# An encoder trunk on one core: wide products with channels on the output partitions, and the residual kept transposed

## The chip, the cores and the metric

The kernel runs on one core of a Trainium2 chip. The metric is the device time of one execution in microseconds; the reference is computed in float32.

## The reference, cut to what matters

The model has two layers (DEPTH 2), 256 tokens, 1024 channels, 2816 hidden channels. In each layer the same residual `x` passes through three parts:

```
h = rms_norm(x, ffn1_norm);  x = x + 0.5 * (silu(h @ w_gate) * (h @ w_up)) @ w_down
h = rms_norm(x, mix_norm)
s5_u, gla_q, gla_k, gla_v, ..., at_q, at_k, at_v = split(h @ w_in)       # three branches
branches = s5(...), gla(...), attn(...)                                   # 512 columns each
merged = sum over b of sigmoid(h @ w_merge_gate[b] + b_merge_gate[b]) * (branch_b @ w_branch_b)
x = x + merged @ w_out
h = rms_norm(x, ffn2_norm);  x = x + 0.5 * (silu(h @ w_gate) * (h @ w_up)) @ w_down
```

After both layers comes a last `rms_norm`. Over 200 MB of weights are read once.

## The kernel before, in words

Every large product goes through `stream`. It walks over blocks of 512 output columns and chunks of four 128-row tiles of the weights. `load` (lines 193 to 214) brings two such row tiles at a time by DMA, and splits each weight into a high part rounded to float32r (ScalarE, line 209) and a low remainder (VectorE, line 210). Activations are split the same way. `mm3` (lines 216 to 221) then makes one product from three matmuls: high by high, high by low, low by high. The activations of 128 tokens are the stationary operand and 512 columns of weights move, so the result has **tokens on the partitions**: two PSUM tiles of 128 tokens x 512 channels per block, and 6 matmuls per row tile of weights and block.

A product that feeds another product must have its channels on the partitions. With tokens on the partitions this takes TensorE transposes (a matmul with the identity), at four places:

- `norm` (lines 251 to 279) transposes the residual `x` (16 transposes of 128x128, line 263), multiplies by the gain (VectorE, line 265), rounds (ScalarE, line 267) and subtracts (VectorE, line 268). The root of the mean square, `rstd`, is one number per token, thus per partition; it is applied when a product leaves PSUM. There are six such norms, and a last one in `final` that needs no transpose.
- `ffn`'s gate/up product: after each block of 256 hidden channels, each of the two token tiles is transposed by itself (line 298), rounded and subtracted (lines 300, 301).
- q and k of the gated linear attention (`ev_tr`, line 714).
- `merge` (line 1127), ahead of the output projection.

The merge gates (lines 748 to 764) add a bias which varies along the free axis, so it is broadcast to all partitions by a DMA (`bm`, line 757). `s5_glu` (lines 876 to 899) is the one product that has channels on the output partitions already: a 128x128 piece of the weights is stationary and 256 tokens move.

The order on each engine is set by a planner of the framework, from its own estimates of durations and the order in which the program is written. Each engine takes its instructions strictly in that order. `weave` mixes the main product stream with side parts (tables of the S5 recurrence, and the three branches).

Of the kernel before, what the change touches and what calls it, by code (L numbers as in the profile page):

```python
# [38 lines left out]
# main steps before a side part begins, and its steps per main step  # L39
# [12 lines left out]
# columns of the constants: those for the mixer, then those for the tables  # L52
# [4 lines left out]
def constants():  # L57
    """Arrays that depend on shapes alone, one row per partition."""
# [24 lines left out]
def cols(*parts):  # L83
    """Columns of weights [K, N] side by side: for the k tiles [a, z)."""
    def f(a, z):
        res, o = [], 0
        for w, cs in parts:
            res.append((w[a * P:z * P, cs].rearrange("(k p) n -> p k n", p=P), 0, o))
            o += cs.stop - cs.start
        return res  # L90
    return f


def weave(main, sides, up=nullcontext):
    """Emit main; from its step `start` on, `per` steps of a side part after each step of main.
    sides: list of [start, per, generator]. Whatever is left of them comes in the end."""
# [29 lines left out]
class Enc:  # L126
    def __init__(self, tc, ctx, ins, out):
# [15 lines left out]
        self.x = c.tile([P, NT, D], F32, name="x")  # L143
        self.cst = c.tile([P, C_MIX], F32, name="cst")
        self.row = {}
        with tc.high_priority():
            self.vectors("ffn1_norm", eng=nc.scalar)
            for h in range(2):
                for t in range(NT):
                    hs = slice(h * 512, (h + 1) * 512)  # L150
                    nc.scalar.dma_start(self.x[:, t, hs], ins["x"][0, t * P:(t + 1) * P, hs])
# [13 lines left out]
    def vectors(self, *names, eng=None):  # L165
        """Parameters of channels, to partitions: [128 channels, (layer, tile)]"""
        nc = self.nc
        eng = eng or nc.sync
        n = 48 if len(names) > 1 else 16
# [3 lines left out]
        for name in names:  # L173
# [6 lines left out]
            else:  # L180
                eng.dma_start(vec[r:r + DEPTH * KD], self.ins[name].rearrange("l (k p) -> (l k) p", p=P))
                self.row[name] = (vt, r, KD)
# [10 lines left out]
    def load(self, pieces):  # L193
        """pieces: list of (dram AP [partitions, k tiles, columns], first partition, first column)"""
# [21 lines left out]
    def mm3(self, ps, act, w, first, last):  # L216
        """act: (hi, lo) [128 k, 128 tok]; w: (hi, lo) [128 k, n]"""
# [4 lines left out]

    def stream(self, act, nk, blocks, lead=1):
        """act(k, t) -> (hi, lo). blocks: list of (pieces(k0, k1) in k tiles, width, evac(t, ps)).
        The first `lead` blocks take their first chunks together."""
# [3 lines left out]
        ps = {}  # L229
        for b, c in order:  # L230
            pieces, width, evac = blocks[b]
            k0, k1 = chunks[c]
            w = self.load(pieces(k0, k1))
            for t in range(NT):
# [6 lines left out]
            for s in range(0, k1 - k0, SUB):  # L241
                for t in range(NT):
                    for k in range(k0 + s, min(k1, k0 + s + SUB)):
                        self.mm3(ps[b, t][:, :width], act(k, t), w[k - k0], k == 0, k == nk - 1)
            if c == len(chunks) - 1:
                for t in range(NT):
                    evac(t, ps[b, t][:, :width])
            yield

# [1 line left out]
    def norm(self, name, l):  # L251
# [3 lines left out]
        sq = self.st.tile([P, 2, NT], F32, name=f"sq{self.n}", tag="sq")  # L255
# [3 lines left out]
        for c in range(2):  # L259
            for t in range(NT):  # L260
# [4 lines left out]
                nc.vector.tensor_tensor(f, pt, g[:, 4 * c:4 * c + 4].unsqueeze(2).to_broadcast((P, 4, P)), op=ALU.mult)  # L265
                h = hi[:, 4 * c:4 * c + 4, t * P:(t + 1) * P]
                nc.scalar.copy(h, f)  # L267
                nc.vector.tensor_tensor(lo[:, 4 * c:4 * c + 4, t * P:(t + 1) * P], f, h.bitcast(F32), op=ALU.subtract)  # L268
        for c in range(2):
            for t in range(NT):  # L270
                junk = self.t2([P, 512])
                nc.scalar.activation(junk, self.x[:, t, c * 512:(c + 1) * 512], AF.Square,
                                     accum_out=sq[:, c, t:t + 1])
        ms = self.st.tile([P, NT], F32, name=f"ms{self.n}", tag="ms")
        nc.vector.tensor_tensor(ms, sq[:, 0], sq[:, 1], op=ALU.add)
        nc.vector.tensor_scalar(ms, ms, 1.0 / D, EPS, op0=ALU.mult, op1=ALU.add)
        nc.gpsimd.tensor_tensor(rstd, ms, self.mhalf[:, :NT], op=ALU.pow)
        act = lambda k, t: (hi[:, k, t * P:(t + 1) * P], lo[:, k, t * P:(t + 1) * P])
        return act, rstd

    def ffn(self, l, which):
        nc, ins = self.nc, self.ins
        wg, wu, wd = (ins[f"{which}_w_{s}"][l] for s in ("gate", "up", "down"))
        with self.tc.tile_pool(name=f"ffn{which}{l}", bufs=1) as fp:
            self.phase, self.rings = fp, {"ra": 4}
            act, rstd = self.norm(f"{which}_norm", l)
            sh = fp.tile([P, KF, SEQ], F32R, name=f"sTh{which}{l}")
            sl = fp.tile([P, KF, SEQ], F32R, name=f"sTl{which}{l}")

            def evac(b):  # L290
                def f(t, ps):
                    self.n += 1
# [884 lines left out]
```

## Time and profile before

| | |
|---|---|
| time, median of 3 runs | 1378.12 us (1378.01 to 1379.51) |
| span of the profiled execution | 1376.2 us |
| the profiled execution's own time beside its span | not listed; the median of the runs is 1.9 us above the span |
| PE / DVE / ACT busy | 97% / 74% / 51% |
| matmuls, and as many weight loads | 6920 |
| DMA, mean share of 16 engines | 57.5% in the main queue |

PE is TensorE, PEld its weight loads, DVE is VectorE, ACT is ScalarE, POOL is GpSimd. A matmul's duration in the trace includes its way through the array, which overlaps the next one, so the distance from start to start says what a matmul costs in a sequence.

### The profile page before, as it was taken

How to read it: one execution, taken by the hardware profiler on the slowest of the kernel's cores; microseconds unless marked ns; L12 is line 12 of the kernel's file. 1: busy time of each engine (PE TensorE's matmuls, PEld its weight loads, DVE VectorE, ACT ScalarE, POOL GpSimd, SP SyncE). 2: the span in 40 equal slices, each digit the busy share in tenths (PEclk: the TensorE clock that was granted, in tenths of full speed). 3: DMA queues.
4: the chain of work that ended last, by engine and by line, in shares of the span. 5: the costliest groups of instructions: out<-in, count | busy, mean ns of one | idle time of the engine just before them, and what ended most of it. 6: DMA issues, size and time to landing. Idle time of an engine off the chain costs nothing.

```text
span 1376.2 us, 19506 instructions
## 1 busy us (share of the span) xinstructions
PE 1336.0 (97%) x6920; PEld 1061.6 (77%) x6920; DVE 1018.4 (74%) x1826; ACT 698.6 (51%) x1102; POOL 73.5 (5%) x104
## 2 busy tenths in 40 slices
PE   7999999999999999999999999999999999999997
PEld 5878788778787678768877777887787877888886
DVE  5899975779986789996465775457799767655553
ACT  5545345447585355445355454354475754555542
POOL 1020210000100000110000000000001000000000
PEclk9999999999999999999999999999999999999999
DMA  7766666565453366666665646566654533655662
GB/s 227 195 211 224 234 222 179 189 205 198 140 183 122 107 161 206 200 202 221 198 195 173 204 149 204 180 178 202 196 200 134 168 107 122 191 178 186 182 213 76
DMA packets 201201, 249.88 MB, mean 182 GB/s; under 512 B 40856, under 2 KB 134600, under 8 KB 201104
## 3 DMA queue, kind: packets, MB, share of 16 engines
q1 hardware_dynamic: 200496, 247.59, 57.5%
q8 instruction: 54, 0.88, 0.3%
q10 hardware_dynamic: 608, 1.06, 0.2%
q14 instruction: 43, 0.35, 0.1%
HBM read 234.44 MB, written 13.11 MB: 180 GB/s over the span
## 4 chain that ended last, share of the span: by engine, by line
PE 63%; issue 17%; DVE 13%; DMA 3%; ACT 3%; POOL 1%; SPq 0%; POOLq 0%; ACTq 0%; DVEq 0%
PE mm L220 18%; PE mm L219 17%; PE mm L221 17%; DVE lo L210 4%; PE S L818 1%; DMA raw<-in_ffn_w_gate 1%; DMA raw<-in_ffn_w_up 1%; PE as L1070 1%; ACT hi L209 1%; PE ao L1092 1%; DVE t L349 1%; PE st L298 1%; DVE run L836 1%; DVE run L835 1%; PE apt L1085 1%
## 5 line engine op out<-in xcount | busy, mean ns | idle before, releaser
L210 DVE TENSOR_TENSOR lo<-raw,hi 128x1024 fp32r<-128x1024 f32 x412 | 499.4, 1217 | 191.7 <-ACT hi L209 184.1
L209 ACT CAST hi<-raw 128x1024 fp32r<-128x1024 f32 x412 | 427.7, 1042 | 305.6 <-PE mm L221 276.3
L220 PE MATMUL mm<-lo,hTh 128*128 128x512 f32 (+1 forms) x1120 | 445.3, 398 | 5.3 <-DVE lo L210 4.9
L219 PE MATMUL mm<-hi,hTh 128*128 128x512 f32 (+1 forms) x1120 | 437.6, 396 | 2.7 <-ACT hTh L267 2.7
L221 PE MATMUL mm<-hi,hTl 128*128 128x512 f32 (+1 forms) x1120 | 436.1, 392 | 0.0
L220 PEld LDWEIGHTS mm<-lo,hTh 128*128 128x128 f32 x1120 | 211.2, 189 | 51.7 <-DVE lo L210 9.2
L219 PEld LDWEIGHTS mm<-hi,hTh 128*128 128x128 f32 x1120 | 211.2, 189 | 45.5 <-ACT hTh L267 3.8
L221 PEld LDWEIGHTS mm<-hi,hTl 128*128 128x128 f32 x1120 | 210.6, 188 | 40.6 <-DVE hTl L268 0.3
L220 PE MATMUL mm<-lo,sThffn 128*128 128x512 f32 x352 | 138.9, 395 | 2.0 <-DVE lo L210 2.0
L221 PE MATMUL mm<-hi,sTlffn 128*128 128x512 f32 x352 | 138.1, 393 | 0.0
L219 PE MATMUL mm<-hi,sThffn 128*128 128x512 f32 x352 | 136.4, 395 | 0.0
L300 ACT CAST sThffn<-st 128x256 fp32r<-128x256 f32 x88 | 32.6, 372 | 128.7 <-PE st L298 128.5
L220 PEld LDWEIGHTS mm<-lo,sThffn 128*128 128x128 f32 x352 | 66.4, 189 | 16.6 <-DVE lo L210 2.5
L221 PEld LDWEIGHTS mm<-hi,sTlffn 128*128 128x128 f32 x352 | 66.5, 189 | 14.1
L219 PEld LDWEIGHTS mm<-hi,sThffn 128*128 128x128 f32 x352 | 66.5, 189 | 13.8
L301 DVE TENSOR_TENSOR sTlffn<-st,sThffn 128x256 fp32r<-128x256 f32 x88 | 36.9, 421 | 50.3 <-ACT sThffn L300 49.9
L294 ACT ACTIVATE t<-mm,rstd 128x256 f32<-128x256 f32 x88 | 41.6, 475 | 43.0 <-PE mm L221 40.2
L295 DVE SCALAR_TENSOR_TENSOR t<-mm,rstd,t 128x256 f32<-128x256 f32 x88 | 41.4, 479 | 12.6 <-ACT t L294 12.4
L818 PEld LDWEIGHTS S<-U,bb 64*128 64x128 f32 x256 | 24.6, 187 | 12.8 <-issue 11.2
L298 PE MATMUL st<-ident,t 128*128 128x128 f32 x176 | 33.4, 272 | 0.0
L298 PEld LDWEIGHTS st<-ident,t 128*128 128x128 f32 x176 | 24.4, 140 | 11.3
L349 DVE TENSOR_TENSOR t<-e,S 128x256 f32<-128x256 f32 x64 | 22.4, 414 | 12.7 <-DMA e<-scr 6.9
(355 smaller groups left out, 1452.6 us busy)
## 6 DMA issues: line engine op xcount, KB each, us to landing
raw<-in_ffn_w_gate SPq DMA_DIRECT2D x176, 256.0 KB, 3.7
raw<-in_ffn_w_up SPq DMA_DIRECT2D x176, 256.0 KB, 4.4
raw<-in_ffn_w_down SPq DMA_DIRECT2D x88, 512.0 KB, 4.6
raw<-in_w_in SPq DMA_DIRECT2D x48, 512.0 KB, 4.4
raw<-in_w_merge_gate SPq DMA_DIRECT2D x48, 512.0 KB, 3.8
raw<-in_w_out SPq DMA_DIRECT2D x16, 512.0 KB, 4.6
scr<-e SPq DMA_DIRECT2D x6, 768.0 KB, 3.7
e<-scr SPq DMA_DIRECT2D x6, 768.0 KB, 5.7
```

The costliest lines, as they stand in the source:

```text
L209: nc.scalar.copy(hi[:, :e - s, :width], raw[:, :e - s, :width])
L210: nc.vector.tensor_tensor(lo[:, :e - s, :width], raw[:, :e - s, :width], hi[:, :e - s, :width].bitcast(F32), op=ALU.subtract)
L219: nc.tensor.matmul(ps, act[0], w[0], start=first, stop=False)
L220: nc.tensor.matmul(ps, act[0], w[1], start=False, stop=False)
L221: nc.tensor.matmul(ps, act[1], w[0], start=False, stop=last)
L294: nc.scalar.activation(sg, ps[:, :256], AF.Silu, scale=rstd[:, t:t + 1])
L295: nc.vector.scalar_tensor_tensor(s, ps[:, 256:], rstd[:, t:t + 1], sg, op0=ALU.mult, op1=ALU.mult)
L298: nc.tensor.transpose(pt[:, j], s[:, j * P:(j + 1) * P], self.ident)
L300: nc.scalar.copy(h, pt)
L301: nc.vector.tensor_tensor(sl[:, 2 * b:2 * b + 2, t * P:(t + 1) * P], pt, h.bitcast(F32), op=ALU.subtract)
L349: self.nc.vector.tensor_tensor(out, a, b, op=ALU.mult)
L818: nc.tensor.matmul(S[g][:, r, a * 64:(a + 1) * 64], bb[rows, a, r], U[rows, pair[a]], start=True, stop=True)
```

## The change

The residual is held as `xT`, with channels on the partitions. All wide products but gate/up and those with narrow or token-major use (u, v, the attention's q, k and v, the swish gate) are computed by `mm3T`: a 128x128 piece of the weights is stationary and all 256 tokens move. Two output tiles of 128 channels share a PSUM bank; only the first matmul in a bank clears it, and the second tile's first matmul is kept behind it. `norm` reads `xT` without transposes (but for the first one). The sum of squares over channels now runs over partitions: squares on ScalarE, sums on GpSimd, a small matmul with ones. The root must now vary along the free axis: a diagonal matrix of `rstd` is multiplied by ones on TensorE and copied to `root`. The gates' bias becomes one number per partition, and goes into the activation. Gate/up keeps tokens on the partitions, but both token tiles are transposed together. The down product of the last layer's second FFN stays as it was; `to_tokens` transposes `xT` back ahead of it.

The core of the diff:

```diff
+    def mm3T(self, ps, act, w, first, last, after=None):
+        nc = self.nc
+        m = nc.tensor.matmul(ps, w[0], act[0], start=first and after is None, stop=False, skip_group_check=True)
...
+        nc.tensor.matmul(ps, w[0], act[1], start=False, stop=False, skip_group_check=True)
+        nc.tensor.matmul(ps, w[1], act[0], start=False, stop=last, skip_group_check=True)
+        return m
...
+                for j, pair in enumerate(pairs):
+                    for i, n in enumerate(pair):
+                        for k in ks:
+                            wk = [x[:, n * P:(n + 1) * P] for x in w[k - k0]]
+                            m = self.mm3T(ps[b, j][:, i * SEQ:(i + 1) * SEQ], act(k), wk, k == 0, k == nk - 1,
+                                          cleared[b, j] if k == 0 and i else None)
...
     def norm
-        for c in range(2):
-            for t in range(NT):
-                pt = self.ptr.tile([P, 4, P], F32, name=self.nm("pt"), tag="tr")
-                for k in range(4):
-                    nc.tensor.transpose(pt[:, k], self.x[:, t, (4 * c + k) * P:(4 * c + k + 1) * P], self.ident)
-                f = self.t2([P, 4, P])
...
+        for j, src in self.to_channels() if first else ((j, self.xT[:, 2 * j:2 * j + 2]) for j in range(KD // 2)):
+            for i in range(2):
+                k = 2 * j + i
+                nc.scalar.activation(hi[:, k], src[:, i], AF.Copy, scale=g[:, k:k + 1])
+                nc.vector.scalar_tensor_tensor(lo[:, k], src[:, i], g[:, k:k + 1], hi[:, k].bitcast(F32),
+                                               op0=ALU.mult, op1=ALU.subtract)
...
+        sums = self.t2([P, 2, SEQ])
+        for j in range(KD // 2):
+            s = self.t2([P, 2, SEQ]) if j else sums
+            nc.scalar.activation(s, self.xT[:, 2 * j:2 * j + 2], AF.Square)
+            if j:
+                nc.gpsimd.tensor_tensor(sums, sums, s, op=ALU.add)
+        nc.gpsimd.tensor_tensor(sums[:, 0], sums[:, 0], sums[:, 1], op=ALU.add)
+        pm = self.ptr.tile([P, NT, 2], F32, name=self.nm("pm"), tag="tr")
+        for t in range(NT):
+            nc.tensor.matmul(pm[:, t], sums[:, 0, t * P:(t + 1) * P], self.ones[:, :2], start=True, stop=True)
...
         nc.gpsimd.tensor_tensor(rstd, ms, self.mhalf[:, :NT], op=ALU.pow)
+        for t in range(NT):
+            nc.vector.tensor_scalar(dg[:, t], self.ident, rstd[:, t:t + 1], None, op0=ALU.mult)
+        pr = self.ptr.tile([P, SEQ], F32, name=self.nm("pr"), tag="tr")
+        nc.tensor.matmul(pr, self.ones, dg.rearrange("p t i -> p (t i)"), start=True, stop=True)
...
+        nc.scalar.copy(self.root, pr)
...
     ffn, evac of gate/up
+                    if t == NT - 1:
+                        pt = self.ptr.tile([P, 2, NT, P], F32, name=self.nm("st"), tag="tr")
+                        for j in range(2):
+                            for i in range(NT):
+                                nc.tensor.transpose(pt[:, j, i], rows[i][:, j * P:(j + 1) * P], self.ident)
+                        fs = slice(2 * b, 2 * b + 2)
+                        self.split_into(sh[:, fs], sl[:, fs], pt.rearrange("p j i t -> p j (i t)"))
...
     mixer: q and k
-                    row = self.t2([P, 512], ring="rg")
-                    nc.scalar.activation(row, ps, AF.Copy, scale=rstd[:, t:t + 1])
...
+                return lambda j, ps: self.by_root(dst[:, 2 * j:2 * j + 2], ps)
...
     gate_stream
-            bm = self.mp.tile([P, 512], F32, name=self.nm("bm"), tag="bm")
-            nc.sync.dma_start(bm, b[i * D + c * 512:i * D + (c + 1) * 512].unsqueeze(0).to_broadcast((P, 512)))
...
+                self.by_root(gates[i][:, k:k + 2], ps)
+                for k in (k, k + 1):
+                    g = gates[i][:, k]
+                    nc.scalar.activation(g, g, AF.Tanh, scale=0.5, bias=bias[:, i * KD + k:i * KD + k + 1])
...
     merge
-                for k in range(4):
-                    nc.tensor.transpose(pt[:, k], gates[0][:, t, (4 * c + k) * P:(4 * c + k + 1) * P], self.ident)
...
+        for j in range(KD // 2):
+            ks = slice(2 * j, 2 * j + 2)
+            self.split_into(mh[:, ks], ml[:, ks], gates[0][:, ks])
...
+    def to_tokens(self):
+        for c in range(2):
+            for t in range(NT):
+                pt = self.ptr.tile([P, 4, P], F32, name=self.nm("xt"), tag="tr")
+                for k in range(4):
+                    nc.tensor.transpose(pt[:, k], self.xT[:, 4 * c + k, t * P:(t + 1) * P], self.ident)
+                nc.scalar.copy(self.x[:, t, c * 512:(c + 1) * 512], pt)
```

`by_root` multiplies a product by `root`, `add_half` adds half of it to `xT`, one VectorE instruction of 128x512 each.

## Rows read from the trace of the kernel before

**Rows 1.** The page's part 1: busy time, share of the span, instructions.

```profile
PE 1336.0 (97%) x6920; PEld 1061.6 (77%) x6920; DVE 1018.4 (74%) x1826; ACT 698.6 (51%) x1102; POOL 73.5 (5%) x104
```

**Rows 2.** The page's part 4: the chain that ended last, by engine and line.

```profile
PE 63%; issue 17%; DVE 13%; DMA 3%; ACT 3%; POOL 1%; SPq 0%; POOLq 0%; ACTq 0%; DVEq 0%
PE mm L220 18%; PE mm L219 17%; PE mm L221 17%; DVE lo L210 4%; PE S L818 1%; DMA raw<-in_ffn_w_gate 1%; DMA raw<-in_ffn_w_up 1%; PE as L1070 1%; ACT hi L209 1%; PE ao L1092 1%; DVE t L349 1%; PE st L298 1%; DVE run L836 1%; DVE run L835 1%; PE apt L1085 1%
```

**Rows 3.** Groups by line and shape: busy us, mean ns of one | idle before, releasers.

```profile
L220 PE MATMUL mm<-lo,hTh 128*128 128x512 f32 x1088 | 436.0, 401 | 5.3 <-DVE lo L210 4.9
L220 PE MATMUL mm<-lo,sThffn 128*128 128x512 f32 x352 | 138.9, 395 | 2.0 <-DVE lo L210 2.0
...
L263 PE MATMUL pt<-ident,x 128*128 128x128 f32 x96 | 16.5, 309 | 9.5 <-DVE t L265 6.3 <-DMA x<-in_x 3.2
...
L1127 PE MATMUL mT<-ident,gate 128*128 128x128 f32 x32 | 5.0, 278 | 2.0 <-DVE mTl L681 1.6 <-DVE gate L352 0.3
L714 PE MATMUL qkT<-ident,t 128*128 128x128 f32 x32 | 4.7, 279 | 0.0
```

**Rows 4.** Timeline of PE, last down product: first and last of 33 matmuls (start, length).

```profile
1360.10 0.39 PE L219 MATMUL mm<-hi,sThffn 128*128 128x512 f32 x1
...
1367.42 0.40 PE L221 MATMUL mm<-hi,sTlffn 128*128 128x512 f32 x1
```

**Rows 5.** Timeline of PE, the S5 GLU of both layers: ends of three unbroken stretches.

```profile
407.74 0.28 PE L887 MATMUL glu<-ysh,hi 128*128 128x256 f32 x1
...
408.10 0.28 PE L887 MATMUL glu<-ysh,hi 128*128 128x256 f32 x1
...
410.64 0.28 PE L887 MATMUL glu<-ysh,hi 128*128 128x256 f32 x1
...
411.66 0.28 PE L887 MATMUL glu<-ysh,hi 128*128 128x256 f32 x1
...
1093.55 0.28 PE L889 MATMUL glu<-ysh,lo 128*128 128x256 f32 x1
...
1094.69 0.28 PE L887 MATMUL glu<-ysh,hi 128*128 128x256 f32 x1
...
1097.87 1.13 PE L1070 MATMUL as<-akT,aqT 64*128 64x256 f32 x4
```

**Rows 6.** Timeline of PE, layer 1, from the mixer to the second FFN.

```profile
1178.92 1.04 PE L263 MATMUL pt<-ident,x 128*128 128x128 f32 x8
1180.56 1.25 PE L263 MATMUL pt<-ident,x 128*128 128x128 f32 x8 [0.60 <-DVE t L265]
...
1182.81 0.40 PE L220 MATMUL mm<-lo,hTh 128*128 128x512 f32 x1
```

**Rows 7.** Timeline of PE and DVE, layer 0, from the mixer to the second FFN.

```profile
495.86 1.03 PE L263 MATMUL pt<-ident,x 128*128 128x128 f32 x8
...
497.62 1.22 DVE L355 TENSOR_TENSOR wa<-wraw,wa 32x1024 fp32r<-32x1024 f32 x1 [1.37 <-ACT wa L655]
...
505.24 0.50 PE L221 MATMUL mm<-hi,hTl 128*128 128x512 f32 x1
```

**Rows 8.** Timeline of PE, layer 0, from the last branch to the output projection.

```profile
470.14 0.60 PE L1127 MATMUL mT<-ident,gate 128*128 128x128 f32 x4
...
475.30 0.47 PE L221 MATMUL mm<-hi,mTl 128*128 128x512 f32 x1
```

**Rows 9.** Groups by line and shape: VectorE in the norms, GpSimd at 128x512.

```profile
L265 DVE TENSOR_TENSOR t<-pt,vecT 128x512 f32<-128x512 f32 x24 | 16.0, 681 | 2.8 <-PE pt L263 2.8
L268 DVE TENSOR_TENSOR hTl<-t,hTh 128x512 fp32r<-128x512 f32 x24 | 15.9, 682 | 0.8 <-ACT hTh L267 0.7
...
L617 POOL TENSOR_TENSOR e<-r,tcst 128x512 f32<-128x512 f32 x8 | 16.8, 2103 | 127.4 <-DVE r L349 79.7 <-DMA scr<-e 27.1 <-DMA raw<-in_ffn_w_down 11.0
```

**Rows 10.** Windows at two seams: each engine's busy us, PEclk, DMA share, GB/s.

```profile
494.00:506.00 12.00, 8.69 (x39) 6.63 (x39) 9.81 (x20) 6.98 (x14) 0.00 (x0) 0.86 0.65 150
1178.00:1184.00 6.00, 5.40 (x31) 4.19 (x30) 6.00 (x10) 3.40 (x5) 0.00 (x0) 1.00 0.59 187
```

More of the change, by code (lines that the diff above doesn't have):

```diff
@@ L180, in vectors @@
             else:
-                eng.dma_start(vec[r:r + DEPTH * KD], self.ins[name].rearrange("l (k p) -> (l k) p", p=P))
-                self.row[name] = (vt, r, KD)
+                rows = self.ins[name].rearrange("l (k p) -> (l k) p", p=P)
+                eng.dma_start(vec[r:r + rows.shape[0]], rows)
+                self.row[name] = (vt, r, self.ins[name].shape[1] // P)
             r += DEPTH * self.row[name][2]
@@ L228, in stream @@
         order += [(b, c) for b in range(lead, len(blocks)) for c in range(len(chunks))]
-        ps = {}
+        ps, cleared = {}, {}
         for b, c in order:
-            pieces, width, evac = blocks[b]
+            pieces, width, evac, *pairs = blocks[b]
+            pairs = pairs[0] if pairs else None
             k0, k1 = chunks[c]
             w = self.load(pieces(k0, k1))
-            for t in range(NT):
+            for t in range(len(pairs) if pairs else NT):
                 if c == 0:
@@ L274, in norm @@
         ms = self.st.tile([P, NT], F32, name=f"ms{self.n}", tag="ms")
[L275 to L276 removed]
+        nc.vector.tensor_scalar(ms, pm[:, :, 0], 1.0 / D, EPS, op0=ALU.mult, op1=ALU.add)
         nc.gpsimd.tensor_tensor(rstd, ms, self.mhalf[:, :NT], op=ALU.pow)
[L278 to L279 removed]
@@ L281, in ffn @@
-    def ffn(self, l, which):
+        dg = self.st.tile([P, NT, P], F32, name=self.nm("dg"), tag="dg", bufs=1)
+        for t in range(NT):
+            nc.vector.tensor_scalar(dg[:, t], self.ident, rstd[:, t:t + 1], None, op0=ALU.mult)
+        pr = self.ptr.tile([P, SEQ], F32, name=self.nm("pr"), tag="tr")
+        nc.tensor.matmul(pr, self.ones, dg.rearrange("p t i -> p (t i)"), start=True, stop=True)
+        self.root = self.st.tile([P, SEQ], F32, name=self.nm("root"), tag="root", bufs=1)
@@ new lines, in norm, with parts, act, by_root @@
+        nc.scalar.copy(self.root, pr)
+        return self.parts(hi, lo), rstd
+    def parts(self, hi, lo):
+        def act(k, t=None):
+            ts = slice(0, SEQ) if t is None else slice(t * P, (t + 1) * P)
+            return hi[:, k, ts], lo[:, k, ts]
+        return act
+    def by_root(self, out, ps):
+        self.mul(out, ps, self.root.unsqueeze(1).to_broadcast((P, 2, SEQ)))
+    def add_half(self, c):
+        def f(j, ps):
+            xs = self.xT[:, 4 * c + 2 * j:4 * c + 2 * j + 2]
+            self.nc.vector.scalar_tensor_tensor(xs, ps, 0.5, xs, op0=ALU.mult, op1=ALU.add)
+        return f
@@ L282, in ffn @@
+    def ffn(self, l, which, first=False, last=False):
         nc, ins = self.nc, self.ins
@@ L309, in ffn @@
             yield from self.stream(act, KD, blocks, lead=2)
+            sact = self.parts(sh, sl)
+            if not last:
+                yield from self.stream(sact, KF, [(cols((wd, slice(c * 512, (c + 1) * 512))), 512, self.add_half(c),
+                                                   ((0, 1), (2, 3))) for c in range(2)])
+                return
             def down(c):
@@ L708, in ev_tr @@
             def ev_tr(dst):
-                def f(t, ps):
-                    row = self.t2([P, 512], ring="rg")
-                    nc.scalar.activation(row, ps, AF.Copy, scale=rstd[:, t:t + 1])
-                    pt = self.ptr.tile([P, 4, P], F32, name=self.nm("qkT"), tag="tr")
-                    for h in range(4):
-                        nc.tensor.transpose(pt[:, h], row[:, h * P:(h + 1) * P], self.ident)
-                    nc.scalar.copy(dst[:, :, t * P:(t + 1) * P], pt)
-                return f
+                return lambda j, ps: self.by_root(dst[:, 2 * j:2 * j + 2], ps)
             def ev_g(t, ps):
@@ L1146, in run @@
         self.mixer(1)
-        weave(self.ffn(1, "ffn2"), [])
-        self.final()
+        with self.tc.tile_pool(name="xout", bufs=1) as xp:
+            self.x = xp.tile([P, NT, D], F32, name="x")
+            weave(self.ffn(1, "ffn2", last=True), [[4, 1, self.to_tokens()]])
+            self.final()
 def tile_encoder(tc, ins, out):
```

137 lines of the change are left out of this document (69 added, 68 removed).

## The prediction

> **What bounds the kernel now.** I read the busy times first [rows 1]: PE works 97% of the span, and the next engine, DVE, 74%. That alone proves little, since a matmul's length includes its way through the array. So I read the chain that ended last [rows 2]: lines 219 to 221, the three matmuls of the wide products, hold 52% of it, and "issue", 17%, is time in which PE waits for nothing that the profile shows; no other engine has more than 13%. The table of groups [rows 3] shows almost no idle time ahead of the wide matmuls (5.3 us ahead of 1088 of them). The kernel is as long as PE's list of instructions, plus short stalls at the seams between stages. So the price of an edit is what PE's own list gains or loses, from start to start, and what a seam gains or loses.
>
> Two unit prices come from the timeline. In the last down product 33 matmuls of 512 columns start between 1360.10 and 1367.42 [rows 4]: 7.32 / 32 = 0.2288 us each. A transpose: 8 take 1.04 us from first start to last end, one alone 0.28 [rows 3, 6], so (1.04 - 0.28) / 7 = 0.109 us each.
>
> **Part 1, transposes that go.** Of the 96 in the norms only the first norm's 16 stay; the 32 of q and k and the 32 of the merge go [rows 3]. `to_tokens` adds 16. Net 80 + 32 + 32 - 16 = 128, at 0.109 us: **-14.0 us**. In gate/up there are as many transposes as before, four together in place of two and two; VectorE and ScalarE read them in one instruction in place of two. PE gains nothing there, so I set it to 0. The norm's gain multiplication on DVE (0.681 us x 4 per norm) [rows 9] and the bias broadcasts go; DVE and the DMA are not the bound, so 0 too.
>
> **Part 2, the seams.** From the mixer to the second FFN of layer 1, 3.89 us pass between the first transpose and the matmul at 1182.81 [rows 6]. In them are 16 transposes (1.75 us) and five wide matmuls (1.14 us); the other 1.0 us is waiting, for DVE, which is busy 6.00 of 6.00 us there [rows 10]. The order is: add to `x`, transpose, multiply, round, subtract. Afterwards the multiplication and rounding are one ScalarE instruction straight from `xT`, and the half of the channels whose product ended a block earlier can be prepared while PE is busy; its 48 matmuls (11 us) then cover the other half. At the three seams that follow an FFN I take 1.0 us of waiting each to vanish: -3.0. At the two that follow a mixer the buffer of the normed activations is held by the output projection until its last matmul, so a rounding must still pass: 0.2 us gained in layer 1. In layer 0 the seam takes 9.38 us [rows 7], of which 16 transposes and eight wide matmuls are 3.6; the remaining 5.8 us come from an instruction for the gates' small weights (line 355), queued on DVE ahead of the seam's work and late itself, and from a half-speed clock behind the stall (PEclk 0.86 over the window) [rows 10]. That queueing isn't touched by the change; I take half of what is beyond a 1.0 us rounding: -2.4. Between the last branch and the output projection 5.16 us pass [rows 8] with 12 transposes and eight wide matmuls (3.14): 2.0 us of waiting, twice. The split now reads `gates[0]` directly and half of it is ready early: -1.75 each, -3.5. Sum: **-9.1 us**. Bounds: 0 (DVE's chain simply takes the transposes' place) and -13.8 (all of 4 x 1.0 + 5.8 + 2 x 2.0).
>
> **Part 3, the shape.** For each 128 x 512 piece of weights, 6 matmuls of 512 columns become 12 of 256. Pieces: three down products of 22 row tiles x 2 blocks (132; 3/4 of the 352 matmuls that each line has there [rows 3]), and per layer q and k 16, gates 48, branches 24, output 16 (208 in all). 340 x 6 = 2040 matmuls become 4080. Their price is in the trace, since the S5 GLU already has this form [rows 5]: 9 intervals in 1.02 us (0.1133), 10 in 1.14 (0.114), 3 in 0.36 (0.12). I take 0.116, between the long stretches and the slow one. A pair then costs 0.232 against 0.2288: 2040 x 0.0032 = **+6.5 us**. Bounds: 0.1133 gives -4.5, 0.12 gives +22.8.
>
> The rows also show loads of weights as often as matmuls, and twice as many would follow from this part: PEld is busy 1061.6 us [rows 1], 0.189 us per load by its mean. The Trainium skill ("Trainium Kernel Development and Optimization", Performance Expectations) says to judge TensorE by the busy share of its weight loads, not by that of its matmuls. By that rule this change spends what is short. Here the GLU's loads start as often as its matmuls, so they overlap one another and the sum of their lengths bounds nothing; by the row the term stays at +6.5. The rule's outcome is a rival below.
>
> **Part 4, new small products.** Each of six norms gets two matmuls of two columns and one float32 matmul of 256. For the latter the nearest row is line 1070's, four in 1.13 us; with 0.39 for one alone [rows 4], (1.13 - 0.39) / 3 = 0.25 [rows 5]. With two at a transpose's price (0.22) and a change of operand type on either side, which I estimate at 0.1 us each, a norm pays 0.7: **+4.2 us**; bounds +2 and +6. Their chain lies beside other work: the sums on GpSimd take three additions of 128x512 at 2.1 us [rows 9] and one of half the size; with the squares, two PE steps, the power and the copy some 12 us pass, while the first product of the new stage leaves PSUM after three chunks of 24 matmuls, 16.5 us (14 in the mixer, whose second block is narrow). If that cover were gone, the first evacuation would wait.
>
> **Sum.** -14.0 - 9.1 + 6.5 + 4.2 = -12.4 us. The span of 1376.2 becomes 1363.8, and with the 1.9 us between span and median **1366 us**. From the bounds of parts 2 to 4 the forecast's own range is 1348 to 1393; their ends hardly meet, so some 1355 to 1376.
>
> **Rivals.**
> *PE waits in its own queue for GpSimd.* PE takes instructions in order. The two-column matmul is placed where the planner believes the sums to be done. If it believes in faster additions than 2.1 us (the eight that the trace has are of tables, not of a norm [rows 9]), PE stands still, with every wide matmul behind it. An error of 1.3 us per addition over three is 4 us, six times: +24, result 1390. It decides from 12.4 / 6 = 2.1 us per norm. For it: the planner has let PE stall before, behind line 355 [rows 7]. Against it: no PE instruction waited on GpSimd before, so nothing shows such an error. Chance 0.12.
> *The seams stay.* DVE is full at the seam [rows 10]; if its chain sets the seam's length, the transposes removed there (112 of 144) only make room for waiting. Then -3.5 for q and k, +1.7 for `to_tokens`, +6.5, +4.2: +8.9, result 1387. Against it: DVE loses 2.7 us of work per norm. Chance 0.11.
> *The weight loads bind.* 2040 more at 0.189 are +386 us on 1061.6 [rows 1], less 128 of the transposes at no more than that: at least 1423, more than the span. Result at least 1425. The skill's rule named above speaks for it; the overlapping loads in the GLU speak against it. Chance 0.04.
> *Slow stretch everywhere.* 0.12 per matmul: +22.8 in place of +6.5, result 1382. Chance 0.05.
> *Everything at its fast end.* 0.1133 and all seams emptied: 1350. Chance 0.10.
>
> **How the numbers follow.** The forecast has 0.58. A difference under 0.2% (2.8 us) is about what a measurement of this kernel can't tell from none. Faster: the forecast but for 0.02, and the fast end, 0.66. Same: 0.02 of the forecast, and what the GpSimd and seam rivals give at a third of their price, 0.08. Slower: the rest, 0.26. The range 1350 to 1390 leaves out the weight loads, half of the fast end and the worse part of the GpSimd stall, under 0.2.
>
> **What would show it.** Line 263 x16 and no lines 714 and 1127 (part 1). At the seams wide matmuls within 1 us of the last of the stage before (part 2). In the gates and down products, starts 0.113 to 0.12 us apart (part 3). No PE idle time with GpSimd or the sums as releaser (part 4). The prediction is wrong if 256-column matmuls in long runs cost over 0.119 us, or if PE stands before the small products by over 2 us per norm.

## The result: 1395.5 us, slower by 1.4%

The changed kernel takes 1395.48 us (median of 4 runs, 1393.84 to 1403.14) against 1378.45 in the same comparison: ratio 1.0139, 95% interval 1.0111 to 1.0166. The forecast of 1366 and its range up to 1390 both miss, on the wrong side. The execution that was profiled is the longest of the four (1403.14; span 1401.0, 24.8 more than before), so sums over the trace have to explain 24.8 us and not the 17.0 between the medians.

The page's part 1 and the wide groups of part 5 after the change; they answer to [rows 1, 3].

```profile
PE 1358.4 (97%) x8868; PEld 1178.9 (84%) x8868; DVE 1026.3 (73%) x1802; ACT 695.2 (50%) x1076; POOL 136.2 (10%) x129
...
L233 PE MATMUL mm<-sThffn,lo 128*128 128x256 f32 x528 | 149.4, 285 | 6.0 <-DVE lo L210 6.0
L227 PE MATMUL mm<-sThffn,hi 128*128 128x256 f32 x528 | 150.4, 286 | 0.0
L233 PE MATMUL mm<-hTh,lo 128*128 128x256 f32 x512 | 147.9, 292 | 2.0 <-DVE lo L210 2.0
```

Groups by line and shape, the transposes and small products that are left:

```profile
L289 PE MATMUL pt<-ident,xin 128*128 128x128 f32 x16 | 3.4, 354 | 3.3 <-DMA xin<-in_x 3.3
L317 PE MATMUL pm<-ones,t 128*128 128x2 f32 x24 | 3.0, 230 | 0.0
L407 PE MATMUL xt<-ident,xT 128*128 128x128 f32 x16 | 2.4, 273 | 0.0
```

The page's 97% is the same as before and says nothing. What was to go is gone: 16 transposes are left in the norms and 16 in `to_tokens`, none for q, k and the merge. The small products wait for nothing (0.0 us idle ahead of `pm`), so GpSimd's sums never held PE.

Timeline of PE at the seams, a line each for the last matmul of a stage and the first of the next: first FFN to mixer, last branch to output product, mixer to second FFN in layer 0 and in layer 1 ([rows 6 to 8] before).

```profile
228.02 0.28 PE L233 MATMUL mm<-sThffn,lo 128*128 128x256 f32 x1
228.14 0.40 PE L219 MATMUL mm<-hi,hTh 128*128 128x512 f32 x1
...
489.10 0.28 PE L233 MATMUL mm<-yah,lo 128*128 128x256 f32 x1
489.22 0.52 PE L227 MATMUL mm<-mTh,hi 128*128 128x256 f32 x3
...
512.36 0.28 PE L233 MATMUL mm<-mTh,lo 128*128 128x256 f32 x1
514.12 0.50 PE L219 MATMUL mm<-hi,hTh 128*128 128x512 f32 x1 [1.48 <-ACT hTh L302]
...
1202.29 0.28 PE L233 MATMUL mm<-mTh,lo 128*128 128x256 f32 x1
1204.04 0.50 PE L219 MATMUL mm<-hi,hTh 128*128 128x512 f32 x1 [1.48 <-ACT hTh L302]
```

Two of the same seams before, first FFN to mixer and mixer to second FFN in layer 0:

```profile
216.14 0.39 PE L221 MATMUL mm<-hi,sTlffn 128*128 128x512 f32 x1
...
218.56 0.50 PE L219 MATMUL mm<-hi,hTh 128*128 128x512 f32 x1
...
495.63 0.39 PE L221 MATMUL mm<-hi,mTl 128*128 128x512 f32 x1
...
500.86 0.60 PE L219 MATMUL mm<-hi,hTh 128*128 128x512 f32 x1
```

The gain was real. Over the seven seams the time from the last start of a stage to the first of the next was 20.2 us in the trace before (2.4 + 2.9 + 2.8 after an FFN, 5.2 + 2.9 after a mixer, 2.0 + 2.0 before an output product). It is now 4.1: five seams of 0.12 and two of 1.75, where PE waits for ScalarE's rounding of the normed activations. Of the 112 transposes that went there, 82 stood in these 20.2 us; the other 30 stood among the wide matmuls on either side.

So where did the loss come in? First the price of a start. Timeline of PE in the first FFN's down product, the first and the last of 25 matmuls:

```profile
225.14 0.28 PE L233 MATMUL mm<-sThffn,lo 128*128 128x256 f32 x1
...
228.02 0.28 PE L233 MATMUL mm<-sThffn,lo 128*128 128x256 f32 x1
```

24 intervals in 2.88 us are 0.120 each, and so it is in nearly every long stretch (0.120 at the 10th and the 90th percentile); only the branches are at 0.113 to 0.118 (mean 0.115). Second, three stalls in the timeline of PE:

```profile
57.37 0.52 PE L653 MATMUL cT<-ident,U 128*128 128x128 f32 x3 [3.93 <-DMA bn<-in_s_b_im]
...
175.27 0.58 PE L233 MATMUL mm<-sThffn,lo 128*128 128x256 f32 x1 [4.99 <-DVE lo L210]
...
253.47 0.76 PE L881 MATMUL uT<-ident,up 64*128 64x64 f32 x5 [2.25 <-DVE up L873]
```

Third, the granted clock. Windows of PE over the products with q, k and the gates in both mixers (columns: busy us, granted clock as a share of full speed, DMA share, GB/s), the kernel before first and then the changed one:

```profile
218.60:419.00 200.40, 197.57 (x1159) 1.00 0.57 179
901.90:1102.00 200.10, 196.84 (x1158) 1.00 0.56 179
```

```profile
318.20:328.40 10.20, 10.20 (x28) 0.50 0.36 103
228.10:437.40 209.30, 207.00 (x1531) 0.95 0.55 166
919.00:1122.90 203.90, 200.63 (x1515) 0.97 0.57 170
```

Before, the engine had its 2.4 GHz throughout. After, there are stretches at 1.2 GHz (0.50), one of 10.2 us. The time that a clock below 1.00 can cost is (1 - share) x length: 0.05 x 209.3 + 0.03 x 203.9 = 16.6 us, against 0. It is the most that the clock can cost, in this one execution. The forecast had no term for it. I use this number, "lost by clock in the mixers", for the runs below; two decimals make it good to about 1 us in each window.

### The profile page after: what moved, and what is told of

Its sections match the earlier page's. It is cut to its first block, busy times and chain, and to the rows that moved or that the text cites. A ratio compares the mean times of both kernels' runs of the same rounds, so it can differ in the third digit from the quotient of the medians.

```text
span 1401.0 us, 23365 instructions
## 1 busy us (share of the span) xinstructions
PE 1358.4 (97%) x8868; PEld 1178.9 (84%) x8868; DVE 1026.3 (73%) x1802; ACT 695.2 (50%) x1076; POOL 136.2 (10%) x129
## 5 line engine op out<-in xcount | busy, mean ns | idle before, releaser
L219 PE MATMUL mm<-hi,hTh 128*128 128x512 f32 x864 | 342.5, 400 | 5.0 <-ACT hTh L302 5.0
L220 PE MATMUL mm<-lo,hTh 128*128 128x512 f32 x864 | 344.7, 399 | 2.1 <-DVE lo L210 1.8
L221 PE MATMUL mm<-hi,hTl 128*128 128x512 f32 x864 | 337.9, 395 | 1.3 <-DVE hTl L303 1.3
L233 PE MATMUL mm<-sThffn,lo 128*128 128x256 f32 x528 | 149.4, 285 | 6.0 <-DVE lo L210 6.0
L227 PE MATMUL mm<-sThffn,hi 128*128 128x256 f32 x528 | 150.4, 286 | 0.0
L233 PE MATMUL mm<-hTh,lo 128*128 128x256 f32 x512 | 147.9, 292 | 2.0 <-DVE lo L210 2.0
L232 PE MATMUL mm<-sTlffn,hi 128*128 128x256 f32 x528 | 149.8, 284 | 0.0
L232 PE MATMUL mm<-hTl,hi 128*128 128x256 f32 x512 | 149.7, 293 | 0.0
L227 PE MATMUL mm<-hTh,hi 128*128 128x256 f32 x512 | 149.4, 292 | 0.0
L227 PEld LDWEIGHTS mm<-sThffn,hi 128*128 128x128 f32 x528 | 101.8, 193 | 0.5
L774 DVE TENSOR_TENSOR sTlffn<-st,sThffn 128x512 fp32r<-128x512 f32 x44 | 30.2, 685 | 56.5 <-ACT sThffn L773 56.5
```

The source lines that it names most:

```text
L219: nc.tensor.matmul(ps, act[0], w[0], start=first, stop=False)
L220: nc.tensor.matmul(ps, act[0], w[1], start=False, stop=False)
L221: nc.tensor.matmul(ps, act[1], w[0], start=False, stop=last)
L227: m = nc.tensor.matmul(ps, w[0], act[0], start=first and after is None, stop=False, skip_group_check=True)
L232: nc.tensor.matmul(ps, w[0], act[1], start=False, stop=False, skip_group_check=True)
L233: nc.tensor.matmul(ps, w[1], act[0], start=False, stop=last, skip_group_check=True)
```

## The experiments

Theory 1: the price of a 256-column start (0.120) is the loss. Theory 2: the planner's new order of PE's list, with its stalls and the clock behind them. All ratios are to the kernel before on the same chip.

**Does the place in memory set the price?** In the compiled change, weights and activations start 64 bytes into a line of 128, but for the branches and the last down product, where the activations start at 0. `aligned` moves all of it by 64 bytes; `apart` moves only what lies behind the weights; `late_side` keeps the places and starts the woven parts later. A fourth run, `before_shift`, gives the kernel before the padding of `aligned`.

```diff
 aligned, in the constants:  +        c.tile([P, 16], F32, name="pad")
 apart, behind the weights:  +        pool("gap", 1).tile([P, 16], F32, name="gap")
 late_side:  -RATES = (3, 2.5, 10, 2.0, 14, 1.75)
             +RATES = (4, 2.5, 11, 2.0, 15, 1.75)
```

> The changed kernel with 64 bytes of padding among the constants, so that all later tiles move by 64 bytes; every engine's list of instructions is the same. In the changed kernel the weights' parts and the normed activations lie 64 bytes off a multiple of 128, and their 256-column matmuls start 0.120 us apart; in the branches, where the activations lie on a multiple and the weights off it, 0.113 to 0.118. Here weights and activations (hT, mT, most of sT) lie on multiples of 128, the branches' activations off. Theory 'both off a line are slow': 3500 matmuls fall from 0.120 to about 0.115, -17 us, about 1377. Theory 'weights and activations at the same place in a 128-byte line are slow': 0.120 stays, about 1394. Theory 'the shape in long runs is slow wherever it lies': 0.120 stays, about 1394.

> The changed kernel with 64 bytes between the weights' parts and the activations: weights stay 64 bytes off a multiple of 128, normed activations come onto one, the branches' activations go off. Same lists of instructions. Both theories of addresses: hT, mT and sT products at about 0.115, branches at 0.120: about 1379. Theory 'the shape in long runs': 0.120 stays, about 1394.

> The changed kernel with the three side parts of the mixer starting one step of the product stream later (4, 11, 14+1 in place of 3, 10, 14). Theory 'stalls of the order': in the changed kernel PE waits 2.3 and 1.3 us ahead of the S5's transposes for the round trip of u, and its clock is at half speed for 6.8 us behind each; with 5 us more of products in between both go, and the time falls by 5 to 12 us, to 1383 to 1390. Rival: the planner's new order has stalls of its own elsewhere, 1394 within 4.

Measured: 1397.49 (1.011 [1.0079, 1.0141]), 1399.11 (1.014 [1.012, 1.0161]) and 1422.27 (1.0308 [1.0286, 1.033]). In `aligned` 256 columns stay at 0.120. In `apart` they fall, and 512 columns rise. Its timeline of PE, the ends of 27 and of 16 matmuls:

```profile
908.75 0.28 PE L228 MATMUL mm<-sThffn,hi 128*128 128x256 f32 x1
...
911.81 0.28 PE L234 MATMUL mm<-sThffn,lo 128*128 128x256 f32 x1
```

```profile
745.17 0.39 PE L220 MATMUL mm<-hi,hTh 128*128 128x512 f32 x1
...
748.67 0.39 PE L220 MATMUL mm<-hi,hTh 128*128 128x512 f32 x1
```

3.06 / 26 = 0.1177 and 3.50 / 15 = 0.2333, against 0.120 and 0.2285. So the place matters, by 2%, in opposite directions for the two lengths, and the sum gains nothing. The last down product agrees: its 512 columns fall from 0.2289 to 0.2267 in `apart`, where its activations come to the weights' place. `before_shift` was expected at 1378 if only the 256-column shape minds a shift of everything, and at 1398 if 512 columns do too; it took 1380.94 (1.0009 [0.9999, 1.0019]). `late_side`'s expectation (a gain) failed by 32 us: a small shift of the order alone can cost 27 us over the change. Order is worth more than any term of the forecast.

**Undoing one part of the change.** `qk_old` has the q/k blocks as before, `evac_old` gate/up's transposes (two and two, as before), `mix_old` q/k, gates, branches and merge; `resid_old` is the kernel before with just these new.

```diff
 qk_old:    -(cols((w, c(512, 1024))), 512, ev_tr(m["qT"]), ((0, 1), (2, 3))),
            +(cols((w, c(512, 1024))), 512, ev_tr(m["qT"])),
 evac_old:  -if t == NT - 1:
            -    pt = self.ptr.tile([P, 2, NT, P], F32, name=self.nm("st"), tag="tr")
            ...
            +pt = self.ptr.tile([P, 2, P], F32, name=f"st{self.n}", tag="tr")
```

> The changed kernel with q and k of the gated linear attention as before (tokens on the partitions, 512 columns, transposed). Theory 'price': a piece of 128 x 512 weights costs 0.067 us more as twelve matmuls at 0.120 than as six at 0.2288; 32 pieces are 2.2 us, the 32 transposes saved are 3.5, so the kernel gets 1.3 us slower than the changed one, about 1396. Theory 'order and clock': the S5's small matmuls are put one by one between these 256-column matmuls, half the wide work stands between two of them, and the clock falls to half speed there (10.2, 6.8 and 3.4 us in the two mixers); with 512 columns back it stays up, 5 to 12 us less than the changed kernel, 1384 to 1391.

> The changed kernel with gate/up's two token tiles transposed one by one, as before. Price: nothing, 1395. If the joint transposes delay the down products or hold buffers (the first FFN of layer 0 stands 4.3 us before the tables' transposes and 5.3 us in its down product), 3 to 9 us less.

> The changed kernel with q, k, the merge gates, the branches and the merge's transposes as before, and no root row; the residual, the norms, the down and the output product stay as in the change. Price: 176 pieces give back 9 us (the branches' 48 at 0.116 nearly nothing), 64 transposes, two seams and the root chain take 12 to 13: 1396 to 1399. Order and clock: the products of the mixer up to the gates took 8.9 and 3.8 us longer in the changed kernel than before, and those go, 1384 or below.

> The other half alone: q, k, gates, branches and merge as in the change, with a root row made from the mixer's rstd; the residual, norms, down, output product and gate/up as before. Price: 164 pieces (11 us) go, 64 transposes and the seams' waiting (12 us) come back: about 1396. If the mixer's order carries the loss, it stays above 1388; if the FFN stages carry it (they took 5.4, 4.6, 4.0 and 2.5 us longer), it comes to about 1380.

Measured: 1385.91 (1.0056 [1.0037, 1.0074]), 1384.56 (1.0038 [1.0015, 1.006]), 1392.21 (1.0087 [1.0063, 1.0111]), 1389.43 (1.0071 [1.0047, 1.0095]). Undoing q/k gives 9.6 us back where prices say that it costs 1.3; lost by clock in the mixers falls from 16.6 to 6.2. Undoing gate/up's transposition, priced at 0, gives 10.9 back: 6.5 of it by that clock (10.1 left), and the first FFN of layer 0, where the stalls at 57 and 175 us were, is 8.4 us shorter in the profiled execution. (Each taken against its own kernel before, 10.7 and 12.0 us come back; for gate/up 3 to 9 were expected.) The ten executions of `qk_old` show the clock in the time: they lie between 1382.4 us at a mean clock of 0.992 and 1392.3 at 0.987. Theory 1 doesn't survive as the whole. But `mix_old` missed both of its expectations, 1396 and 1384: with q, k and the gates back at 512 columns it gives back 3.3 us, less than `qk_old` alone, and still loses 7.9 us by clock in the mixers. `resid_old`, with the change in the mixers alone, stays above the 1388 that its expectation set for a loss in the mixer's order, and loses 14.6 us by clock there.

**Is undoing additive, and what does each part do alone?** `both_old` undoes both; `norm_only` is the change without new q/k, gates, branches, merge and gate/up; `evac_new` is the kernel before with gate/up's joint transposition alone.

> The changed kernel with both the q/k blocks and gate/up's transposition as before the change; each alone gave some 10 us back. Theory 1 (prices alone): +1.3 us for q and k and 0 for the transposition, 1396 to 1398. Theory 2 (each part's order costs by itself, and the costs add): 1374 to 1377, faster than the kernel before. Theory 3 (the stalls are set by chance of the order, so that each undoing draws a new order of about the same quality): 1380 to 1390.

> The kernel before with the norms, the residual kept with channels on partitions, the down products and the output product as in the change; q/k, gates, branches, the merge's transposes and gate/up's transposition as before. 80 - 16 transposes go (-7.0 us), 164 pieces have the new shape (984 matmuls, +11.3 us at 0.120 a half), seams as measured in the changed kernel (some -7 us), small products +2 to +4: by prices 1377 to 1382. If the order of the first FFN with the joint transposition was the loss in the kernel that kept the old mixer parts (1392.2), this one is 8 to 12 us faster than that one; if the loss there was the order of the rest, it stays at 1390.

> The kernel before with one part of the change alone: gate/up's product is transposed for all 256 tokens at once (four transposes into one bank, read by one ScalarE and one VectorE instruction), everything else as before. Theory 1 (prices alone): the same number of transposes, 0 us, 1379 to 1381. Theory 2 (the joint transposition makes the first FFN of layer 0 longer by its order and by stalls in which the granted clock falls): +4 to +11, 1384 to 1390, with the gate/up and down stages of the first FFN, where the tables' small work is woven in, longer by 5 us or more, and the other FFNs by 1 us or less.

Measured: 1380.83 (1.0014 [1.0004, 1.0025]), 1383.21 (1.003 [1.0015, 1.0045]), 1375.47 (0.9974 [0.9964, 0.9984]). The two do not add up (14.7 of 20.5 us), so a part of it is a new draw of the order. `norm_only` differs from `mix_old` by gate/up's transposition alone and is 9.0 us faster, as its expectation had it for the case that the joint transposition was the loss there. `evac_new` answers to neither theory: the part that cost 11 us inside the change gains 2.8 alone. It is the one version that beats both kernels. Which stage gains can't be said: the products with q, k and the gates are 6 to 8 us shorter and the branches longer by nearly as much, and the rest moves by some 2 us or less.

**The shape alone.** `split` is the kernel before, in which the 2040 matmuls of 512 columns are issued as two of 256 each; nothing else in the program is changed, though the planner makes a new order of it, and the activations stay the stationary operand. `split_qk`, `split_gates` and `split_down` do it for q and k, for gates and branches, and for the three down and the output products.

```diff
+    def halves(self, ps, act, w, first, last):
...
+        for i, (x, y) in enumerate(((0, 0), (0, 1), (1, 0))):
+            for h in range(2):
+                c = slice(h * 256, (h + 1) * 256)
+                m = nc.tensor.matmul(ps[:, c], act[x], w[y][:, c], start=first and i == 0 and h == 0,
+                                     stop=last and i == 2, skip_group_check=True)
```

> The kernel before, in which the 2040 matmuls of 512 columns that the change turns over (the two q/k blocks, gates, branches, output product and three down products) are each issued as two of 256 columns into the two halves of the same bank. The transposes, the norms, the residual and all evacuations stay. This is the shape of part 3 alone. Theory 1 (a start-to-start price of 0.120 us for 256 columns against 0.2285 for 512 is the main loss): 2040 x 0.0115 = +23.5 us, 1400 to 1405, and the page shows 0.120 between most starts. By the price of the prediction (0.116): +6.5, 1386. Theory 2 (the loss is the planner's new order, and shape costs little): 1379 to 1388.

> The kernel before with only the q and k products (192 matmuls of 512 columns) issued as halves of 256. Theory 1 (the price alone): 192 x 0.0115 = +2.2 us, 1380 to 1382. Theory 2 (half-length matmuls among S5's small ones let the granted clock fall in the mixers): half-speed stretches of 10 us or more in the first 120 us of one or both mixers, and +8 to +14 us, 1386 to 1393.

> The kernel before with only the gate and branch products (576 and 288 matmuls of 512 columns) issued as halves of 256. Theory 1 (price): 576 x 0.0115 + 288 x 0.0045 = +7.9 us, 1385 to 1388. Theory 2 (clock): if the gates stand among S5's and attention's small matmuls too, half-speed stretches in the mixers and +12 us or more, 1390 or more; if S5's stretch is q/k's time alone, as theory 1.

> The kernel before with only three down products and the output products (984 matmuls of 512 columns) issued as halves of 256. Nothing small stands among them but for the tables' work in the first FFN. Both theories: the price alone, 984 x 0.0115 = +11.3 us, 1389 to 1392; +3.0 us in each down stage and +1.1 in each output product, and no half-speed stretch in them. If the measured loss is under 5 us, the price itself is not what the starts show.

| kernel | median us | ratio to before | price at 0.120 | lost by clock in the mixers |
|---|---|---|---|---|
| split | 1408.55 | 1.0205 [1.0187, 1.0223] | +23.5 | 21.6 |
| split_qk | 1398.86 | 1.014 [1.012, 1.016] | +2.2 | 20.8 |
| split_gates | 1383.39 | 1.0036 [1.0023, 1.0049] | +7.9 | 4.0 |
| split_down | 1383.08 | 1.0027 [1.0017, 1.0038] | +11.3 | 0 |

The shape alone costs more than the whole change, and its parts add up: 20.6 + 5.1 + 4.8 = 30.5 against 30.2 us. Price and clock together don't: they say 45 us for `split`, 11.9 for `split_gates` and 11.3 for `split_down`, over twice what the last two lose. `split` and `split_qk` came out above all of their ranges, `split_gates` below all, and `split_down` 6 us below its own: it lost less than the 5 us at which its expectation gave the price up. Stage by stage the price is there in `split_down`: the down stages of the trace grow by 2.3, 3.0 and 2.2 us and the output products by 1.1 each (a down product at 0.120: 264 x 0.0115 = 3.0); that the whole loses only 4.8 goes with a second FFN whose gate/up product is 4 us shorter in layer 0. What the new orders of `split_gates` and `split` save, I didn't separate. But q and k, a tenth of the matmuls, are two thirds of the loss. Windows of PE in `split_qk`, and then its timeline where the clock falls (L229 issues the halves):

```profile
263.80:272.20 8.40, 8.40 (x31) 0.61 0.68 198
265.70:275.90 10.20, 10.20 (x41) 0.50 0.56 177
959.10:966.60 7.50, 7.50 (x30) 0.69 0.67 177
218.10:427.50 209.40, 204.20 (x1248) 0.95 0.55 171
912.90:1118.80 205.90, 200.49 (x1238) 0.95 0.56 174
```

```profile
264.19 0.50 PE L229 MATMUL mm<-hi,hTl 128*128 128x256 f32 x2
264.62 0.43 PE L834 MATMUL S<-U,bb 64*128 64x64 f32 x2
264.99 0.50 PE L229 MATMUL mm<-hi,hTh 128*128 128x256 f32 x2
265.42 0.46 PE L834 MATMUL S<-U,bb 64*128 64x64 f32 x2
265.81 0.79 PE L229 MATMUL mm<-lo,hTh 128*128 128x256 f32 x2
266.53 0.69 PE L834 MATMUL S<-U,bb 64*128 64x64 f32 x2
267.15 0.79 PE L229 MATMUL mm<-hi,hTl 128*128 128x256 f32 x2
```

Here PE alternates pairs of S5's 64-column matmuls with wide ones. A pair takes 0.37 us from start to start (264.62 to 264.99) and, from 266.53 on, 0.62: the clock has halved. In the kernel before, the same stretch, 259.8 to 267.4, has 15 wide matmuls of 512 columns between the pairs; in `split_qk` it has 14 of 256. The planner puts in about as many matmuls, whatever their length, and so half the columns. The window of the kernel before:

```profile
259.80:267.40 7.60, 7.60 (x32) 1.00 0.44 111
```

Such halves hold half of the time at 1.2 GHz in `split_qk`'s mixer products, 20.4 of 40.8 us (10.2 from 265.7 and 10.2 from 962.0; a half of such time counts as lost). Another 10.2 us stand by waits of 2.60 and 2.42 us that the kernel before doesn't have, ahead of S5's transposes of u (at 244.5 and 938.4). The last 10.2 us, from 313.5 and 1009.8, stand where the wide matmuls among S5's have 512 columns, so these don't always keep the clock up. `mix_old` and `norm_only`, whose products with q, k and the gates have no halves, lose 7.9 us each by clock (a share of 0.97 to 0.99). The changed kernel's own stretch of 10.2 us is of this kind, as its timeline shows (L902 is S5's matmul, and 0.62 us pass from 320.15 to 320.77):

```profile
319.43 0.79 PE L220 MATMUL mm<-lo,hTh 128*128 128x512 f32 x1
320.15 0.69 PE L902 MATMUL S<-U,bb 64*128 64x64 f32 x2
320.77 0.79 PE L221 MATMUL mm<-hi,hTl 128*128 128x512 f32 x1
```

**Is it q and k, or what stands among S5's matmuls?** A woven stretch is one in which S5's small matmuls stand among wide ones. `before_late` is the kernel before with the blocks of the mixer's input product in the order u, z, v, attention, gate, q, k; `split_qk_late` is that with q and k halved, `qk_late` the changed kernel in that order. Now the first woven stretch has 512 columns in each, and only the second has q and k.

```diff
-RATES = (3, 2.5, 10, 2.0, 14, 1.75)
+RATES = (3, 2.5, 14, 2.0, 14, 1.75)
... and the q and k blocks at the end of the list
```

> The kernel before with the blocks of the mixer's input product in another order: q and k last (GLA's woven part starts at step 14 in place of 10). Control for the next run: all wide matmuls stay at 512 columns, so by the theory of the half-length matmuls among S5's small ones the granted clock stays at 1.00 in both mixers; the time may be off by some us for the new order, 1378 to 1390.

> The same order of blocks with q and k as halves of 256. If the loss is tied to q and k as such: +18 to +22 us over its control, as before. If it comes from halves among S5's matmuls: the first woven stretch (15 wide matmuls of 512 columns) keeps the full clock and only the second (14 of 256) shows half-speed stretches, so about half the loss, +7 to +13 us over its control. The price alone: +2.2 us.

> The changed kernel with that order of blocks. If halves among S5's matmuls are the loss: the first woven stretch has 512 columns again, the second halves, the mean granted clock rises over the changed kernel's 0.984 to 0.988 or more, 1385 to 1392. If the order as such is the loss, no telling: 1380 to 1420.

Measured: 1398.52 (1.0147 [1.0127, 1.0168]), 1410.02 (1.023 [1.0209, 1.0251]), 1412.06 (1.0233 [1.0204, 1.0263]). The order costs 19 us by itself, beyond the 1378 to 1390 expected, at a clock of 1.00 in the mixers' products, as expected: GLA's work comes later, and its branch product stretches over 40.3 and 38.9 us in place of 21.6. Against its control, halving q and k costs 11.5 us here, and 20.6 in the old order. Windows of PE over the first and the second woven stretch and the product windows, `before_late` and then `split_qk_late`:

```profile
262.00:269.60 7.60, 7.60 (x32) 1.00 0.37 97
294.40:302.00 7.60, 7.60 (x31) 1.00 0.65 203
...
221.10:414.80 193.70, 191.52 (x1107) 1.00 0.59 185
917.10:1109.50 192.40, 189.49 (x1105) 1.00 0.60 186
```

```profile
259.00:266.50 7.50, 7.50 (x31) 1.00 0.37 95
291.30:297.60 6.30, 6.30 (x30) 0.88 0.67 185
296.10:302.90 6.80, 6.80 (x30) 0.50 0.69 213
218.30:418.00 199.70, 198.38 (x1202) 0.97 0.58 180
916.40:1117.40 201.00, 198.48 (x1201) 0.97 0.58 178
```

The first stretch, 512 columns among the pairs, keeps 1.00 in both. The second keeps it with 512 columns and falls with halves, and all the time at 1.2 GHz in `split_qk_late`'s mixer products is among halves. Lost by clock: 0.03 x 199.7 + 0.03 x 201.0 = 12.0 us; with 2.2 for the starts that is 14.2, and the two product windows are 6.0 and 8.6 us longer than the control's. (The medians differ by 11.5, and the two profiled executions by 7.1: other stages are shorter.) So halves among S5's small matmuls do cost the clock in this stretch. In the old order the fit is looser: up to 20.8 by clock, while the product windows grow by 9.0 and 5.8 and the branches behind them by 5.9. `qk_late` (expected 1385 to 1392) missed; the control's order costs 19 us too.

## Why the prediction was wrong

**Part 1 held.** 128 transposes went, and nothing in the trace contradicts 0.109 each. **Gate/up at 0** held as a price and failed as a statement on the time: -2.8 us alone, and its undoing inside the change gives 10.9 back, through the order.

**Part 2 held.** The seams lost 16.1 us, and the 30 transposes beside them are 3.3 more, together 19.4; 112 of the transposes (12.2 at 0.109) and the 9.1 of waiting would have been 21.3. What is left stands after each mixer, 1.48 us of waiting for the rounding, of which the forecast said that it "must still pass" there, and took 1.0 for it, in layer 0 with 2.4 more for the queue behind line 355, which no longer shows.

**Part 4 held.** From start to start `pm` takes 2.2 us and `pr` 1.6, together 3.8, and the wide matmul behind them holds PE 0.1 and 0.2 us longer than in a long stretch (the forecast had 0.1 on either side for a change of operand type, without a row for it): 5.5 against 4.2, within the bounds of 2 to 6. The rival of GpSimd is refuted by the 0.0 us idle ahead of `pm`, "the seams stay" by the seams.

**Part 3 is the step that failed.** It said +6.5 for the shape; the shape alone, in `split`, costs 30.2. First in size: of the GLU's rows [rows 5] I took 0.116, "between the long stretches and the slow one", but the rows of the GLU have their operands at another place in the 128-byte line than the new products (`apart` shows 0.118 for these too). 2040 x (0.240 - 0.2285) = +23.5 in place of +6.5; the rival "slow stretch everywhere" was the case in which this was right, at 0.05. With it alone the forecast would have been 1383.

Second, a term that was missing: the forecast priced a half matmul as if it lay among its own kind, and said nothing of the woven stretches, where PE had kept 2.4 GHz with 512 columns among S5's 64-column matmuls (1.00 in the windows of the kernel before). `split_qk` shows that halving q and k is worth 18 us beyond its price, with the waits and the new order that it brings, and `split_qk_late` that halves in a woven stretch lose the clock where 512 columns kept it. In the change, 16.6 us are lost by clock in the mixers; undoing q/k takes 10.4 of it away and 9.6 us of time. Only a third of the change's 30.6 us at 1.2 GHz there stands among halves (from 280.6 and 966.7); 6.8 stand by the wait at 253 us and 13.6 (from 318.2 and 1017.9) among 512 columns. So the clock in the mixers is a cost of the planner's new order as much as of the halves. In the trace: -16.1 (seams) - 3.3 (transposes beside them) - 3.5 (q/k's transposes) + 1.7 (`to_tokens`) + 5.5 (part 4) + 20.6 (shape, the branches at 0.115) + 16.6 = +21.5, against 24.8 measured. That it closes so well is partly luck: the first FFN of layer 0 is 12.4 us longer without its seam, of which only the down product's 3.0 is in the sum, and other stages gave much of it back; these stalls come and go with the order, and I didn't separate them.

**The weight loads don't bind.** The loads' busy time rose by 117 us (84% of the span) and the time by 17. In `split` it rose to 1189.8 us, and the time by 30; matmuls start every 0.120 us where a load lasts 0.193, so the loads overlap. The Trainium skill ("Trainium Kernel Development and Optimization", Performance Expectations) says of the distance from the roofline: "MFU and LDWEIGHTS busy % are the good metrics". Read as a bound on the time, as the rival read it, no run here bears it out.

**Not settled:** why the planner's order at large is better or worse, as in `late_side`, `evac_new` against `evac_old`, or `before_late`; and what lets the clock fall in the change's own longest stretch at 1.2 GHz (10.2 us, from 318), which stands among S5's matmuls and 512 columns after ten S5 matmuls in a row, and in the like stretches of `split_qk`, `mix_old` and `qk_old`.

## What to carry to other kernels

Price a new shape where it will stand, not where the trace shows it: among its own kind it costs its starts (two halves of 256 are 0.240 us against 0.2285), but in the list that the planner made around it, halving 192 matmuls cost 18 us more, with waits and stretches at 1.2 GHz, half of these among the halves. In a list that a planner orders, read the granted clock of each stage next to its busy time before and after, for busy PE said 97% both times; and run each part of a change alone, since here the part that was priced at nothing was the only one that gained.

## What was not expected of the hardware

The start-to-start time depends on whether weights and activations start at the same place in a 128-byte line: 0.120 us for 256 columns and 0.2285 for 512 at the same place, 0.1177 and 0.2333 at different ones. And with PE busy without a break (7.50 of 7.50 us in `split_qk`'s window at 959 us) the granted clock still fell to 1.2 GHz, where pairs of 64-column matmuls alternate with 256 columns; with 512 columns in the same place it stayed at 2.4 (1.00 in the window of the kernel before), though not in every such place.
